# Rotary embedding on one core: tiles of 6, 5 and 5 positions without TensorE, and one 256 KB strip of a store split over partitions

## The chip, the cores and the metric

The kernel runs on one core of a Trainium2 chip. The metric is the device time of one execution in microseconds (us); lower is better. Five engines of the core appear in this text: TensorE (PE) multiplies matrices, VectorE (DVE) and GpSimd (POOL) work element by element, ScalarE (ACT) copies and scales, and SyncE (SP) issues the loads. The stores are issued from ScalarE's queue. All transfers between HBM and the on-chip memory (SBUF) run on the same 16 DMA engines. PSUM is a second on-chip memory, into which TensorE writes and which DVE and ScalarE can read and write.

## What is computed

`x` has 8 batches of 2048 positions, with 8 heads of 64 float32 values at each position; `cos` and `sin` have 32 values for each position.

```python
def reference(x, cos, sin):
    x1 = x[..., : x.shape[-1] // 2]
    x2 = x[..., x.shape[-1] // 2 :]
    cos = cos[None, :, None, :]
    sin = sin[None, :, None, :]
    out1 = x1 * cos - x2 * sin
    out2 = x1 * sin + x2 * cos
    return np.concatenate([out1, out2], axis=-1)
```

Both halves of a head are multiplied by the same cosines; to this is added the other half times the sine, with a minus sign for the first half. So an element costs two products and one addition. A batch of `x` is 4 MB; 33.6 MB are read and as many written.

## The kernel before

**Tiling.** A batch is laid over the 128 partitions: partition q holds 16 consecutive positions, 512 values each, so a row of 8192 values (32 KB). One SBUF tile `xt` (lines 64 to 71) holds a batch; there are five such buffers (`NBUF = 5`). The results are written over the input in `xt`, and the store reads it from there. The load of batch b+5 therefore has to wait until the store of batch b has landed and frees the buffer (lines 201 and 202).

**Loads and stores.** SyncE issues the loads in order: batch 0 in three parts (4, 4 and 8 positions), the two tables behind the first of them (lines 66 to 70), then one transfer of 4 MB for each batch. ScalarE's queue issues the stores (line 74): batch 0 in shares of 1, 7 and 8 positions, batch 7 in shares of 8, 4 and 4, every other batch in one of 16 (lines 186 to 191).

**Tables.** ScalarE builds `sgn` from the sines, once with a minus sign and once without (lines 89 to 91). The cosines are copied to PSUM as `cos_ps` (line 94) and the sines as `sin_ps` (line 92). `eye` and `neye` (lines 79 to 88 and 93) are an identity matrix and its negative.

**The work on a tile.** `rotate` (lines 115 to 177) works on a tile of 4 positions, of 2 at the beginning of batch 0 and at the end of batch 7 (lines 179 to 184). It comes in three kinds:

- "A", for all tiles but five: GpSimd multiplies the swapped halves by the signed sines into `t2` (line 134); DVE multiplies by the cosines into `t1`, which lies in PSUM and has one buffer (line 141); DVE adds the two into `xt` (line 148).
- "B", for the first tile of batches 2, 4 and 5: the products are the same, but `t1` lies in SBUF, TensorE adds the two by multiplying both with the identity into a PSUM tile `o` (lines 153 and 154), and ScalarE copies the sum to `xt` (line 155).
- "C", for the first tile of batches 1 and 3: DVE makes both products (lines 141 and 158), TensorE adds them with `eye` or `neye` (lines 169 and 170), ScalarE copies (line 174), and GpSimd has no part in it.

`t2` has three buffers, so GpSimd can be up to three tiles ahead of DVE's additions.

**Order.** `keep` holds the instructions of an engine in the order in which the program names them, so each queue is in program order. The loop in lines 193 to 202 goes over the batches and over the tiles of each; a share is stored as soon as the last tile in it is done.

Of the kernel before, what the change touches and what calls it, by code (L numbers as in the profile page):

```python
# [9 lines left out]
@with_exitstack  # L10
def kernel(
    ctx: ExitStack,
    tc: tile.TileContext,
    x: bass.AP,
    cos: bass.AP,
    sin: bass.AP,
    out: bass.AP,
):
    nc = tc.nc
    keep = tc.keep_in_program_order  # L20
    f32 = mybir.dt.float32
    PSUM = bass.MemoryType.PSUM

    B, S, H, D = x.shape
    Dh = D // 2
    P = 128
    HD = H * D
    R = S // P
    ROW = R * HD
    UNIT = 4 * HD  # L30
    NBUF = 5
    C = 512
    last = B - 1

    xv = x.rearrange("b (q r) h d -> b q (r h d)", q=P)
    ov = out.rearrange("b (q r) h d -> b q (r h d)", q=P)
    cos_src = cos.rearrange("(q r) d -> q r d", q=P)
    sin_src = sin.rearrange("(q r) d -> q r d", q=P)

    const_pool = ctx.enter_context(tc.tile_pool(name="const", bufs=1))  # L40
    tab_pool = ctx.enter_context(tc.tile_pool(name="tab", bufs=1, space=PSUM))
    t1_pool = ctx.enter_context(tc.tile_pool(name="t1p", bufs=1, space=PSUM))
    o_pool = ctx.enter_context(tc.tile_pool(name="op", bufs=2, space=PSUM))
    t1s_pool = ctx.enter_context(tc.tile_pool(name="t1s", bufs=2))
    xpool = ctx.enter_context(tc.tile_pool(name="xpool", bufs=NBUF))
    t2_pool = ctx.enter_context(tc.tile_pool(name="t2p", bufs=3))

    cos_sb = t1s_pool.tile([P, R, Dh], f32, tag="t1s", name="cos_sb")
    sin_sb = t1s_pool.tile([P, R, Dh], f32, tag="t1s", name="sin_sb")
    sgn = const_pool.tile([P, R, 2, Dh], f32, tag="sg")  # L50
    eye = const_pool.tile([P, P], f32, tag="eye")
    neye = const_pool.tile([P, P], f32, tag="neye")
    cos_ps = tab_pool.tile([P, R, Dh], f32, tag="cp")
    sin_ps = tab_pool.tile([P, R, Dh], f32, tag="sp")

    xts = {}

    def spans(sizes):
        lo = 0
        for n in sizes:  # L60
            yield lo, n
            lo += n

    def load(b):
        xt = xpool.tile([P, ROW], f32, tag="xt", name=f"xt{b}")
        for lo, n in spans([UNIT, UNIT, 2 * UNIT] if b == 0 else [ROW]):
            keep(nc.sync.dma_start(out=xt[:, lo : lo + n], in_=xv[b, :, lo : lo + n]))  # L67
            if b == 0 and lo == 0:
                keep(nc.sync.dma_start(out=cos_sb, in_=cos_src))  # L69
                keep(nc.sync.dma_start(out=sin_sb, in_=sin_src))  # L70
        xts[b] = xt

    def store(b, lo, n):
        keep(nc.scalar.dma_start(out=ov[b, :, lo : lo + n], in_=xts[b][:, lo : lo + n]))  # L74

    for b in range(NBUF):
        load(b)

    nc.gpsimd.memset(eye, 0.0)  # L79
    nc.gpsimd.affine_select(  # L80
        out=eye,
        in_=eye,
        compare_op=mybir.AluOpType.not_equal,
        fill=1.0,
        base=0,
        pattern=[[-1, P]],
        channel_multiplier=1,
    )
    for lo, hi in ((0, 4), (4, R)):
        keep(nc.scalar.mul(sgn[:, lo:hi, 0, :], sin_sb[:, lo:hi, :], -1.0))  # L90
        keep(nc.scalar.copy(sgn[:, lo:hi, 1, :], sin_sb[:, lo:hi, :]))  # L91
    keep(nc.scalar.copy(sin_ps, sin_sb))  # L92
    keep(nc.scalar.mul(neye, eye, -1.0))
    keep(nc.vector.tensor_copy(cos_ps, cos_sb))  # L94

    def rep(a, n):
        return dataclasses.replace(a, ap=[a.ap[0][:], a.ap[1][:], [0, n], a.ap[-1][:]])

    def swapped(a, nr):
        return dataclasses.replace(  # L100
            a,
            offset=a.offset + Dh,
            ap=[a.ap[0][:], [HD, nr], [D, H], [-Dh, 2], [1, Dh]],
        )

    def signed(a, nr):
        return dataclasses.replace(
            a, ap=[a.ap[0][:], [D, nr], [0, H], [Dh, 2], [1, Dh]]
        )

    kinds = {}
    for b, kind in ((1, "C"), (2, "B"), (3, "C"), (4, "B"), (5, "B")):
        kinds[(b, 0)] = kind

    def rotate(b, lo, n):
        kind = kinds.get((b, lo), "A")
        xt = xts[b][:, lo : lo + n]
        r0 = lo // HD
        nr = n // HD
        xk = xt.rearrange("p (r k d) -> p r k d", r=nr, d=Dh)  # L120
        xu = xt.rearrange("p (g u d) -> p g u d", u=2, d=Dh)
        if kind == "A":
            t1 = t1_pool.tile([P, n], f32, tag="t1")
        else:
            t1 = t1s_pool.tile([P, n], f32, tag="t1s")
        if kind == "C":
            t2 = t1s_pool.tile([P, n], f32, tag="t1s")
        else:
            t2 = t2_pool.tile([P, n], f32, tag="t2")
        t1u = t1.rearrange("p (g u d) -> p g u d", u=2, d=Dh)  # L130
        t2u = t2.rearrange("p (g u d) -> p g u d", u=2, d=Dh)
        if kind != "C":
            keep(
                nc.gpsimd.tensor_mul(  # L134
                    out=t2.rearrange("p (r h u d) -> p r h u d", r=nr, h=H, u=2),
                    in0=swapped(xt, nr),
                    in1=signed(sgn[:, r0 : r0 + nr, :, :], nr),
                )
            )
        keep(  # L140
            nc.vector.tensor_mul(  # L141
                out=t1.rearrange("p (r k d) -> p r k d", r=nr, d=Dh),
                in0=xk,
                in1=rep(cos_ps[:, r0 : r0 + nr, :], 2 * H),
            )
        )
        if kind == "A":
            keep(nc.vector.tensor_add(out=xt, in0=t1, in1=t2))  # L148
        elif kind == "B":
            for j in range(n // C):  # L150
                o = o_pool.tile([P, C], f32, tag="o")
                cs = slice(j * C, (j + 1) * C)
                nc.tensor.matmul(o, eye, t1[:, cs], start=True, stop=False)  # L153
                nc.tensor.matmul(o, eye, t2[:, cs], start=False, stop=True)  # L154
                keep(nc.scalar.copy(xt[:, cs], o))  # L155
        else:
            keep(
                nc.vector.tensor_mul(  # L158
                    out=t2.rearrange("p (r k d) -> p r k d", r=nr, d=Dh),
                    in0=xk,  # L160
                    in1=rep(sin_ps[:, r0 : r0 + nr, :], 2 * H),
                )
            )
            G = C // Dh
            for u in range(2):
                for j in range(n // 2 // C):
                    o = o_pool.tile([P, C], f32, tag="o")
                    gs = slice(j * G, (j + 1) * G)
                    nc.tensor.matmul(o, eye, t1u[:, gs, u, :], start=True, stop=False)  # L169
                    nc.tensor.matmul(  # L170
                        o, eye if u else neye, t2u[:, gs, 1 - u, :], start=False, stop=True
                    )
                    keep(
                        nc.scalar.copy(  # L174
                            xu[:, gs, u, :], o.rearrange("p (g d) -> p g d", d=Dh)
                        )
                    )

    def pieces(b):
        if b == 0:  # L180
            return [2 * HD, 2 * HD, UNIT, UNIT, UNIT]
        if b == last:
            return [UNIT, UNIT, UNIT, 2 * HD, 2 * HD]
        return [UNIT] * 4

    def shares(b):
        if b == 0:
            return [HD, 7 * HD, 2 * UNIT]
        if b == last:
            return [2 * UNIT, UNIT, UNIT]  # L190
        return [ROW]

    for b in range(B):
        done = 0
        outs = list(spans(shares(b)))
        for lo, n in spans(pieces(b)):
            rotate(b, lo, n)
            done = lo + n
            while outs and sum(outs[0]) <= done:
                store(b, *outs.pop(0))  # L200
        if b + NBUF <= last:
            load(b + NBUF)

# [29 lines left out]
```

## Time and profile before

| | |
|---|---|
| time, median of 9 runs | 163.92 us (163.42 to 168.92) |
| time of the profiled execution | 163.92 us, span 162.0 us |
| DVE busy | 140.1 us, 66 instructions |
| POOL busy | 135.8 us, 38 instructions |
| PE busy | 45.9 us, 80 instructions |
| ACT busy | 15.1 us, 27 instructions |
| bytes moved by DMA | 67.64 MB, mean 418 GB/s |
| load queue (q1), store queue (q10) | 49.6% and 48.2% of 16 engines' span |

The span goes from the first to the last instruction; the rest of the time lies around it. The shares of busy time are averages over the whole span: whether an engine sets the time is seen only from what it waits for, stage by stage. Times in the views are counted from the start of the span. In a group of instructions, the columns are line, engine, operation, output and inputs with their shapes and count, then busy time, the mean of one in ns, and the idle time just before them with what ended it. In the chain of waits, a line is start, length and what. In the table by windows, a line is the window, its length, the busy time of PE, PEld, DVE, ACT and POOL with their counts, the granted TensorE clock, the DMA share and the GB/s. In the timeline, a line is start, length, engine, line, operation and operands.

### The profile page before, as it was taken

How to read it: one execution, taken by the hardware profiler on the slowest of the kernel's cores; microseconds unless marked ns; L12 is line 12 of the kernel's file. 1: busy time of each engine (PE TensorE's matmuls, PEld its weight loads, DVE VectorE, ACT ScalarE, POOL GpSimd, SP SyncE). 2: the span in 40 equal slices, each digit the busy share in tenths (PEclk: the TensorE clock that was granted, in tenths of full speed). 3: DMA queues.
4: the chain of work that ended last, by engine and by line, in shares of the span. 5: the costliest groups of instructions: out<-in, count | busy, mean ns of one | idle time of the engine just before them, and what ended most of it. 6: DMA issues, size and time to landing. Idle time of an engine off the chain costs nothing.

```text
span 162.0 us, 440 instructions
## 1 busy us (share of the span) xinstructions
PE 45.9 (28%) x80; PEld 18.5 (11%) x80; DVE 140.1 (86%) x66; ACT 15.1 (9%) x27; POOL 135.8 (84%) x38
## 2 busy tenths in 40 slices
PE   0000000499008930894039802990000000000000
PEld 0000000143003400341024201430000000000000
DVE  0458999999999999999999899999899998999900
ACT  3310000012100310022001400121000000000000
POOL 1199999999999799979995999996999969999100
PEclk9999999999755997589857995699655555555555
DMA  5999998899999999998999999999999999989994
GB/s 194 413 433 505 437 405 380 372 429 510 388 401 441 494 413 388 502 405 388 502 405 396 486 407 405 477 413 421 469 405 453 453 388 461 445 388 433 413 415 172
DMA packets 3457, 67.64 MB, mean 418 GB/s; under 512 B 384, under 2 KB 384, under 8 KB 768
## 3 DMA queue, kind: packets, MB, share of 16 engines
q1 hardware_dynamic: 1728, 34.08, 49.6%
q10 hardware_dynamic: 1728, 33.56, 48.2%
q14 instruction: 1, 0.01, 0.0%
HBM read 34.08 MB, written 33.55 MB: 418 GB/s over the span
## 4 chain that ended last, share of the span: by engine, by line
DMA 46%; DVE 36%; POOL 8%; issue 4%; SPq 1%; ACT 0%; DVEq 0%; POOLq 0%; ACTq 0%
DMA xt<-in_x_dram 24%; DVE t L141 18%; DMA out_dram<-xt 18%; DVE xt L148 16%; POOL t L134 8%; DMA sin_sb<-in_sin_dram 3%; DVE t L158 1%; SPq L69 0%; SPq L67 0%; ACT sgn L91 0%; DVEq L148 0%; ACT sgn L90 0%; POOLq L134 0%; ACTq L74 0%
## 5 line engine op out<-in xcount | busy, mean ns | idle before, releaser
L134 POOL TENSOR_TENSOR t<-xt,sgn 128x2048 f32<-128x2048 f32 (+1 forms) x32 | 135.1, 4250 | 13.9 <-ACT sgn L91 6.0
L141 DVE TENSOR_TENSOR t<-xt,cos_ps 128x2048 f32<-128x2048 f32 (+1 forms) x34 | 73.4, 2166 | 0.8
L148 DVE TENSOR_TENSOR xt<-t,t 128x2048 f32<-128x2048 f32 (+1 forms) x29 | 62.2, 2145 | 6.8 <-POOL t L134 3.8
L153 PE MATMUL o<-t,eye 128*128 128x512 f32 x24 | 15.5, 734 | 25.4 <-DVE t L141 25.4
L169 PE MATMUL o<-t,eye 128*128 128x512 f32 x16 | 11.6, 828 | 37.8 <-DVE t L141 37.8
L154 PE MATMUL o<-t,eye 128*128 128x512 f32 x24 | 14.7, 702 | 0.0
L155 ACT COPY xt<-o 128x512 f32<-128x512 f32 x12 | 7.0, 586 | 45.0 <-PE o L154 45.0
L153 PEld LDWEIGHTS o<-t,eye 128*128 128x128 f32 x24 | 5.6, 247 | 33.7 <-issue 33.7
L174 ACT COPY xt<-o 128x512 f32<-128x512 f32 x8 | 4.7, 586 | 44.4 <-DVE t L141 26.0
L169 PEld LDWEIGHTS o<-t,eye 128*128 128x128 f32 x16 | 3.8, 256 | 42.7 <-POOL t L134 30.5
L154 PEld LDWEIGHTS o<-t,eye 128*128 128x128 f32 x24 | 5.4, 227 | 7.4 <-issue 7.4
L94 DVE COPY cos_ps<-cos_sb 128x512 f32<-128x512 f32 x1 | 0.7, 695 | 6.1 <-DMA cos_sb<-in_cos_dram 6.1
L170 PE MATMUL o<-t,neye 128*128 128x512 f32 x8 | 5.5, 800 | 0.1
L158 DVE TENSOR_TENSOR t<-xt,sin_ps 128x2048 f32<-128x2048 f32 x2 | 4.6, 2281 | 0.0
L170 PE MATMUL o<-t,eye 128*128 128x512 f32 x8 | 4.1, 592 | 0.0
L170 PEld LDWEIGHTS o<-t,neye 128*128 128x128 f32 x8 | 2.2, 290 | 4.2 <-issue 4.2
L170 PEld LDWEIGHTS o<-t,eye 128*128 128x128 f32 x8 | 1.5, 190 | 1.9 <-issue 1.9
L90 ACT ACT_TABLE_LOAD x1 | 1.3, 1283 | 0.7 <-PEq L217 0.7
L90 ACT ACTIVATE sgn<-sin_sb 128x128 f32<-128x128 f32 (+1 forms) x2 | 0.8, 414 | 4.7 <-DMA sin_sb<-in_sin_dram 4.7
L91 ACT COPY sgn<-sin_sb 128x128 f32<-128x128 f32 (+1 forms) x2 | 0.8, 388 | 0.0
L92 ACT COPY sin_ps<-sin_sb 128x512 f32<-128x512 f32 x1 | 0.6, 579 | 0.0
L79 POOL MEMSET eye<- 128x128 f32 x1 | 0.2, 204 | 0.3 <-POOLq L217 0.3
(6 smaller groups left out, 1.0 us busy)
## 6 DMA issues: line engine op xcount, KB each, us to landing
xt<-in_x_dram SPq DMA_DIRECT2D x7, 4096.0 KB, 39.5
out_dram<-xt ACTq DMA_DIRECT2D x6, 4096.0 KB, 28.5
out_dram<-xt ACTq DMA_DIRECT2D x2, 2048.0 KB, 18.9
xt<-in_x_dram SPq DMA_DIRECT2D x2, 1024.0 KB, 5.9
xt<-in_x_dram SPq DMA_DIRECT2D x1, 2048.0 KB, 11.4
out_dram<-xt ACTq DMA_DIRECT2D x2, 1024.0 KB, 8.8
out_dram<-xt ACTq DMA_DIRECT2D x1, 1792.0 KB, 20.3
cos_sb<-in_cos_dram SPq DMA_DIRECT2D x1, 256.0 KB, 4.9
```

What stands on the lines that cost most here:

```text
L90: keep(nc.scalar.mul(sgn[:, lo:hi, 0, :], sin_sb[:, lo:hi, :], -1.0))
L91: keep(nc.scalar.copy(sgn[:, lo:hi, 1, :], sin_sb[:, lo:hi, :]))
L134: nc.gpsimd.tensor_mul(out=t2.rearrange("p (r h u d) -> p r h u d", r=nr, h=H, u=2), in0=swapped(xt, nr), in1=signed(sgn[:, r0 : r0 + nr, ...
L141: nc.vector.tensor_mul(out=t1.rearrange("p (r k d) -> p r k d", r=nr, d=Dh), in0=xk, in1=rep(cos_ps[:, r0 : r0 + nr, :], 2 * H),)
L148: keep(nc.vector.tensor_add(out=xt, in0=t1, in1=t2))
L153: nc.tensor.matmul(o, eye, t1[:, cs], start=True, stop=False)
L154: nc.tensor.matmul(o, eye, t2[:, cs], start=False, stop=True)
L155: keep(nc.scalar.copy(xt[:, cs], o))
L158: nc.vector.tensor_mul(out=t2.rearrange("p (r k d) -> p r k d", r=nr, d=Dh), in0=xk, in1=rep(sin_ps[:, r0 : r0 + nr, :], 2 * H),)
L169: nc.tensor.matmul(o, eye, t1u[:, gs, u, :], start=True, stop=False)
L170: nc.tensor.matmul(o, eye if u else neye, t2u[:, gs, 1 - u, :], start=False, stop=True)
L174: nc.scalar.copy(xu[:, gs, u, :], o.rearrange("p (g d) -> p g d", d=Dh))
```

## The change

All tiles become kind "A": GpSimd makes the sine product, DVE the cosine product and the addition. TensorE, the tiles `o`, the SBUF `t1`, `sin_ps`, `eye` and `neye` are gone. The tables as loaded, `cos_sb` and `sin_sb`, move to the pool of constants. Batch 0 keeps its tiles of 2, 2, 4, 4 and 4 positions; all others are cut in tiles of 6, 5 and 5, so `t1` and `t2` grow to 6 positions. Batch 7 is stored in shares of 6, 5 and 5 positions. Batch 5 (the sixth) is stored in shares of 15 positions and 1, and the share of 1 position (256 KB) goes out in six transfers over 80, 14, 12, 10, 8 and 4 partitions. Loads are as before. No instruction of TensorE's is left but the branches around the kernel.

```diff
-    UNIT = 4 * HD
     NBUF = 5
-    C = 512
...
-    o_pool = ctx.enter_context(tc.tile_pool(name="op", bufs=2, space=PSUM))
-    t1s_pool = ctx.enter_context(tc.tile_pool(name="t1s", bufs=2))
...
-    cos_sb = t1s_pool.tile([P, R, Dh], f32, tag="t1s", name="cos_sb")
-    sin_sb = t1s_pool.tile([P, R, Dh], f32, tag="t1s", name="sin_sb")
+    cos_sb = const_pool.tile([P, R, Dh], f32, tag="cb")
+    sin_sb = const_pool.tile([P, R, Dh], f32, tag="sb")
...
-    eye = const_pool.tile([P, P], f32, tag="eye")
-    neye = const_pool.tile([P, P], f32, tag="neye")
...
-    sin_ps = tab_pool.tile([P, R, Dh], f32, tag="sp")
...
+    loads = {0: [4, 4, 8]}
+    pieces = {0: [2, 2, 4, 4, 4]}
+    stores = {0: [1, 7, 8], 5: [15, 1], last: [6, 5, 5]}
+    strips = {(5, 15): [80, 14, 12, 10, 8, 4]}
...
-    keep(nc.scalar.copy(sin_ps, sin_sb))
-    keep(nc.scalar.mul(neye, eye, -1.0))
...
-        kind = kinds.get((b, lo), "A")
...
+        keep(
+            nc.gpsimd.tensor_mul(
+                out=t2.rearrange("p (r h u d) -> p r h u d", r=n, h=H, u=2),
+                in0=swapped,
+                in1=signed,
             )
+        )
         keep(
             nc.vector.tensor_mul(
-                out=t1.rearrange("p (r k d) -> p r k d", r=nr, d=Dh),
-                in0=xk,
-                in1=rep(cos_ps[:, r0 : r0 + nr, :], 2 * H),
+                out=t1.rearrange("p (r k d) -> p r k d", r=n, d=Dh),
+                in0=xt.rearrange("p (r k d) -> p r k d", r=n, d=Dh),
+                in1=cosines,
             )
         )
-        if kind == "A":
-            keep(nc.vector.tensor_add(out=xt, in0=t1, in1=t2))
-        elif kind == "B":
...
+        keep(nc.vector.tensor_add(out=xt, in0=t1, in1=t2))
...
     for b in range(B):
-        done = 0
-        outs = list(spans(shares(b)))
-        for lo, n in spans(pieces(b)):
+        outs = list(spans(stores.get(b, [R])))
+        for lo, n in spans(pieces.get(b, [6, 5, 5])):
             rotate(b, lo, n)
-            done = lo + n
-            while outs and sum(outs[0]) <= done:
-                store(b, *outs.pop(0))
+            while outs and sum(outs[0]) <= lo + n:
+                so, sn = outs.pop(0)
+                cs = slice(so * HD, (so + sn) * HD)
+                for p0, p1 in spans_of(strips.get((b, so), [P])):
+                    keep(
+                        nc.scalar.dma_start(out=ov[b, p0:p1, cs], in_=xts[b][p0:p1, cs])
+                    )
```

More of the change, by code (lines that the diff above doesn't have):

```diff
@@ L42 @@
     t1_pool = ctx.enter_context(tc.tile_pool(name="t1p", bufs=1, space=PSUM))
-    o_pool = ctx.enter_context(tc.tile_pool(name="op", bufs=2, space=PSUM))
-    t1s_pool = ctx.enter_context(tc.tile_pool(name="t1s", bufs=2))
     xpool = ctx.enter_context(tc.tile_pool(name="xpool", bufs=NBUF))
     t2_pool = ctx.enter_context(tc.tile_pool(name="t2p", bufs=3))
-    cos_sb = t1s_pool.tile([P, R, Dh], f32, tag="t1s", name="cos_sb")
-    sin_sb = t1s_pool.tile([P, R, Dh], f32, tag="t1s", name="sin_sb")
+    cos_sb = const_pool.tile([P, R, Dh], f32, tag="cb")
+    sin_sb = const_pool.tile([P, R, Dh], f32, tag="sb")
     sgn = const_pool.tile([P, R, 2, Dh], f32, tag="sg")
-    eye = const_pool.tile([P, P], f32, tag="eye")
-    neye = const_pool.tile([P, P], f32, tag="neye")
     cos_ps = tab_pool.tile([P, R, Dh], f32, tag="cp")
-    sin_ps = tab_pool.tile([P, R, Dh], f32, tag="sp")
-    xts = {}
+    loads = {0: [4, 4, 8]}
+    pieces = {0: [2, 2, 4, 4, 4]}
+    stores = {0: [1, 7, 8], 5: [15, 1], last: [6, 5, 5]}
+    strips = {(5, 15): [80, 14, 12, 10, 8, 4]}
     def spans(sizes):
@@ L62, in spans, with spans_of @@
             lo += n
+    def spans_of(sizes):
+        for lo, n in spans(sizes):
+            yield lo, lo + n
+    xts = {}
     def load(b):
         xt = xpool.tile([P, ROW], f32, tag="xt", name=f"xt{b}")
-        for lo, n in spans([UNIT, UNIT, 2 * UNIT] if b == 0 else [ROW]):
-            keep(nc.sync.dma_start(out=xt[:, lo : lo + n], in_=xv[b, :, lo : lo + n]))
+        for lo, n in spans(loads.get(b, [R])):
+            cs = slice(lo * HD, (lo + n) * HD)
+            keep(nc.sync.dma_start(out=xt[:, cs], in_=xv[b, :, cs]))
             if b == 0 and lo == 0:
@@ L71, in load @@
         xts[b] = xt
-    def store(b, lo, n):
-        keep(nc.scalar.dma_start(out=ov[b, :, lo : lo + n], in_=xts[b][:, lo : lo + n]))
     for b in range(NBUF):
         load(b)
[L79 to L88, printed above, removed]
     for lo, hi in ((0, 4), (4, R)):
@@ L91 @@
         keep(nc.scalar.copy(sgn[:, lo:hi, 1, :], sin_sb[:, lo:hi, :]))
-    keep(nc.scalar.copy(sin_ps, sin_sb))
-    keep(nc.scalar.mul(neye, eye, -1.0))
     keep(nc.vector.tensor_copy(cos_ps, cos_sb))
[L96 to L103, printed above, removed]
-        )
@@ L106, in signed @@
-    def signed(a, nr):
-        return dataclasses.replace(
-            a, ap=[a.ap[0][:], [D, nr], [0, H], [Dh, 2], [1, Dh]]
-        )
[L111 to L115, printed above, removed]
-        kind = kinds.get((b, lo), "A")
[L117 to L121, printed above, removed]
-        if kind == "A":
[L123 to L138, printed above, removed]
@@ new lines, in rotate @@
+    def rotate(b, lo, n):
+        xt = xts[b][:, lo * HD : (lo + n) * HD]
+        t1 = t1_pool.tile([P, n * HD], f32, tag="t1")
+        t2 = t2_pool.tile([P, n * HD], f32, tag="t2")
+        part = xt.ap[0]
+        swapped = dataclasses.replace(
+            xt,
+            offset=xt.offset + Dh,
+            ap=[part[:], [HD, n], [D, H], [-Dh, 2], [1, Dh]],
+        )
+        s = sgn[:, lo : lo + n, :, :]
+        signed = dataclasses.replace(
+            s, ap=[s.ap[0][:], [D, n], [0, H], [Dh, 2], [1, Dh]]
+        )
+        c = cos_ps[:, lo : lo + n, :]
+        cosines = dataclasses.replace(
+            c, ap=[c.ap[0][:], c.ap[1][:], [0, 2 * H], c.ap[-1][:]]
+        )
[4 more added lines that the diff above has]
+                in1=signed,
@@ L139, in rotate @@
             )
+        )
         keep(
             nc.vector.tensor_mul(
-                out=t1.rearrange("p (r k d) -> p r k d", r=nr, d=Dh),
-                in0=xk,
-                in1=rep(cos_ps[:, r0 : r0 + nr, :], 2 * H),
-            )
-        )
-        if kind == "A":
-            keep(nc.vector.tensor_add(out=xt, in0=t1, in1=t2))
-        elif kind == "B":
[L150 to L171, printed above, removed]
-                    )
[L173 to L193, printed above, removed]
-        done = 0
-        outs = list(spans(shares(b)))
-        for lo, n in spans(pieces(b)):
-            rotate(b, lo, n)
-            done = lo + n
-            while outs and sum(outs[0]) <= done:
-                store(b, *outs.pop(0))
+                out=t1.rearrange("p (r k d) -> p r k d", r=n, d=Dh),
@@ new lines, in rotate @@
+                in0=xt.rearrange("p (r k d) -> p r k d", r=n, d=Dh),
+                in1=cosines,
+            )
+        )
+        keep(nc.vector.tensor_add(out=xt, in0=t1, in1=t2))
+    for b in range(B):
+        outs = list(spans(stores.get(b, [R])))
+        for lo, n in spans(pieces.get(b, [6, 5, 5])):
+            rotate(b, lo, n)
+            while outs and sum(outs[0]) <= lo + n:
[4 more added lines that the diff above has]
+                        nc.scalar.dma_start(out=ov[b, p0:p1, cs], in_=xts[b][p0:p1, cs])
+                    )
```

## The prediction, made before the changed kernel was run

> **What bounds the kernel now.** I read the totals first, then the chain of waits, then the end of the run in short windows, then the busy engines instruction by instruction.
>
> ```profile
> span 162.0 us, 440 instructions
> ...
> PE 45.9 (28%) x80; PEld 18.5 (11%) x80; DVE 140.1 (86%) x66; ACT 15.1 (9%) x27; POOL 135.8 (84%) x38
> ...
> DMA  5999998899999999998999999999999999989994
> ...
> q14 instruction: 1, 0.01, 0.0%
> ```
>
> The DMA row is at 9 or close to it from the second slice to the last but one: the transfers are the resource that is full. DVE and POOL are not far behind, at 86% and 84%.
>
> ```profile
> 62.99 29.58 DMA out_dram<-xt
> ...
> 92.65 39.49 DMA xt<-in_x_dram
> ...
> 132.28 4.52 POOL t L134
> ...
> 152.52 1.23 DVE xt L148
> ```
>
> This is the chain. Batch 2's store is issued at 62.99 and lands at 92.57; this frees a buffer, so batch 7's load is issued at 92.65 and lands at 132.14; only then do POOL and DVE turn to batch 7, and DVE is done at 153.75. So the DMA queues set the pace of the compute, and DVE waits for them.
>
> ```profile
> 158.00:159.00 1.00, 0.00 (x0) 0.00 (x0) 0.00 (x0) 0.00 (x0) 0.00 (x0) 0.50 1.08 459
> 159.00:159.50 0.50, 0.00 (x0) 0.00 (x0) 0.00 (x0) 0.00 (x0) 0.00 (x0) 0.50 0.66 279
> 159.50:160.00 0.50, 0.00 (x0) 0.00 (x0) 0.00 (x0) 0.00 (x0) 0.00 (x0) 0.50 0.28 115
> 160.00:160.50 0.50, 0.00 (x0) 0.00 (x0) 0.00 (x0) 0.00 (x0) 0.00 (x0) 0.50 0.08 33
> ```
>
> The last two numbers are the DMA share and GB/s. The queue is full until 159 although DVE stopped at 153.75: there was a backlog of stores. Then a share of 0.08, about one engine of sixteen, works on alone. The trace's landing marks say the same: of the last store's sixteen marks fifteen fall between 159.68 and 160.25 and one at 161.15. Batch 2's store and batch 5's load, landing near 92.5, have no such straggler (all marks within 0.55); batch 3's, landing near 113, have it. Between them lies the one instruction fetch of the run (q14), at 96.9. So that fetch put one DMA engine some 0.9 us behind, and a full engine never catches up.
>
> **The change, part by part.** The sum is made against the profiled execution: span 162.0, time 163.92, so 1.92 lies outside the span; its time equals the median of the nine runs. The last store lands at 161.15, leaving 0.85 to the span's end, which I keep.
>
> TensorE gone. Three "B" tiles had their addition on TensorE and ScalarE; it returns to DVE as 3 additions of 2.29. Two "C" tiles had sine products on DVE (L158, 2.28); these become additions of 2.29 there, and POOL gets 2 products of 4.52. The 20 ScalarE copies, sin_ps, neye and eye cost nothing now: ScalarE is 9% busy, and the last two constants are made while POOL waits for the sine table until 7.32. So DVE has 16 positions times two passes in every batch.
>
> Tiles of 6, 5 and 5.
>
> ```profile
> L141 DVE TENSOR_TENSOR t<-xt,cos_ps 128x2048 f32<-128x2048 f32 x30 | 68.5, 2292 | 0.7
> ...
> L141 DVE TENSOR_TENSOR t<-xt,cos_ps 128x1024 f32<-128x1024 f32 x4 | 4.9, 1228 | 0.1
> ...
> L134 POOL TENSOR_TENSOR t<-xt,sgn 128x2048 f32<-128x2048 f32 x28 | 125.9, 4522 | 7.9 <-DMA xt<-in_x_dram 5.0 <-DVE xt L148 2.9
> ...
> L134 POOL TENSOR_TENSOR t<-xt,sgn 128x1024 f32<-128x1024 f32 x4 | 9.3, 2346 | 6.0 <-ACT sgn L91 6.0
> ```
>
> ```profile
> 18.80 2.29 DVE L141 TENSOR_TENSOR t<-xt,cos_ps 128x2048 f32<-128x2048 f32 x1
> 21.20 2.29 DVE L148 TENSOR_TENSOR xt<-t,t 128x2048 f32<-128x2048 f32 x1
> 23.52 2.29 DVE L141 TENSOR_TENSOR t<-xt,cos_ps 128x2048 f32<-128x2048 f32 x1
> ...
> 148.59 1.23 DVE L141 TENSOR_TENSOR t<-xt,cos_ps 128x1024 f32<-128x1024 f32 x1
> 149.93 1.23 DVE L148 TENSOR_TENSOR xt<-t,t 128x1024 f32<-128x1024 f32 x1
> 151.19 1.23 DVE L141 TENSOR_TENSOR t<-xt,cos_ps 128x1024 f32<-128x1024 f32 x1
> ```
>
> A round of DVE (product, addition, gaps) takes 23.52 - 18.80 = 4.72 for 4 positions and 151.19 - 148.59 = 2.60 for 2, so 1.06 per position and 0.48 per round. No row shows a tile of 5 or 6 positions. Bounds for a batch: 4 x 4.72 = 18.88 if larger tiles save nothing, 16 x 1.06 = 16.96 if they cost no fixed part at all. I take the line through both rows: 6.84 + 5.78 + 5.78 = 18.40. POOL by its rows: 2.176 per 2 positions and 0.17 fixed, so 6.70 and 5.61; a batch 17.92, less than DVE.
>
> Then I walk the two engines through. Batch 0 keeps its pieces, so DVE ends it at 28.2 as before (the addition at 25.92 plus 2.29). POOL starts batch 1 at 25.6 and needs 6.70, so DVE's first addition waits to 32.3, 0.5 lost. Batch 1 ends at 47.2. From there DVE is never kept waiting: six batches of 18.40 give 65.6, 84.0, 102.4, 120.8, 139.2, 157.6. POOL starts batches 5, 6 and 7 near 97.4, 115.4 and 133.3, after the loads that landed at 92.4, 112.8 and 132.1 before. Before, DVE ended at 153.75; now 3.85 later.
>
> Do the later stores starve the queue? A full queue needed the stores of batches 1 to 6 by 53.6, 73.1, 92.6, 113.0, 132.3 and 141.8 (when its predecessor landed). They come at 47.2, 65.6, 84.0, 102.4, 120.8 and 139.2: all in time, the last by 2.6. So loads keep their times. After load 7 the fifteen punctual engines moved 48 positions in 160.25 - 131.12 = 29.13, which is 0.607 a position. The 43 positions ahead of the last store land by 131.12 + 43 x 0.607 = 157.2. The last store, 5 positions, is issued at 157.6 into an idle queue. That is the new wait: the backlog that hid DVE's end is used up.
>
> Its cost has no row of its own. The first load, on an idle queue, took 4.63 for 4 positions (0.74 to 5.37); one position more gives 5.24, an upper bound, since it also warmed up on reads. Lower bound: 1.0 to the first packet (as the first load), 5 x 0.607 of data, 0.35 from the last packet to landing (as the last store of before): 4.4. I take 4.8: landing at 162.4, so 1.25 later than 161.15.
>
> The instruction fetch. TensorE's stream was the long one; with it the fetch at 96.9 should go, and the straggler's 0.9 with it. This is a gain only for a kernel whose queue is full at the end. Here it shortens the idle stretch and is worth nothing; if the fetch stays, its engine is free near 158.1, still before the last store's data can start (158.6), so again nothing.
>
> The strip. Six transfers of 256 KB in all replace one share of a large store. ScalarE's queue issues at 0.34 each, with nothing behind them until batch 6's store at 139.2; they sit behind batch 5's large part, which lands near 140. All transfers take eight completion semaphores in turn, and each waits for the one eight before it: the sixth strip so waits for load 7 (131 to 132) and batch 6's store for batch 4's; behind them on ScalarE nothing is due before 139.2. Cost from below: nothing, as the gap before the last store hides over a microsecond. From above: five more transfers, each with the first load's whole start (4.63 - 4 x 0.607 = 2.2), 11 us. The nearest row is transfers queued behind each other: cosines, then sines, 256 KB each, landed at 6.03 and 6.71, 0.68 apart, where 0.607 is data. So 0.07 each, 0.35 for five, hidden: I take 0. The Trainium skill (DMA: Bandwidth & Descriptors, Anatomy of one DMA) speaks against the strip: it puts a fixed cost of about 2 us on every DMA, most of it the receipt of the write, and the same page's rules call transfers under 64 KB mostly overhead. Five more would then be an estimated 10 us; the 0.68 between cosines and sines shows no such cost for transfers queued together.
>
> Sum: 163.92 + 1.25 = 165.17, say 165.2.
>
> **The rivals.** Faster: DVE does the larger tiles cheaply, and the queue stays full. It decides if the last store is issued before about 155.7 (drained packets at 156.9, less 1.0 to the first, and 0.2 for the spread of the engines), 1.9 earlier than my 157.6, which asks for a batch in 18.13. Then the kernel ends as now without its straggler: 163.92 - 0.90 = 163.0. For it: DMA is the full resource today. Against it: two sizes of tile lie on a line, and the fixed part that could go is only 0.48 a round.
>
> No change: DVE ends 0.9 to 1.5 sooner than I say, so that the idle gap just eats what the lost straggler gives: 163.6 to 164.25.
>
> Larger tiles save nothing: 18.88 a batch puts DVE's end near 161.0, and the time at 168.6. For it: a scratch tile of 6 positions was never run. Against it: the linear rows.
>
> The strips stall: 11 us between batches 5 and 6 delay the drain to 168.2, and then 5 x 0.607 to a landing at 171.3: 174.0. It decides above about 1.5. Against it stands the 0.68.
>
> **How the numbers follow.** Forecast 0.80: 164.4 (DVE 0.4 sooner, last store 4.4) to 166.1 (DVE 0.5 later, 5.24). Faster rival 0.08, no change 0.06, larger tiles slower 0.04, strips 0.02. Differences under 0.2%, 0.33 us, can't be told from no change. So faster 0.08, same 0.06, slower 0.86. The range 163.9 to 166.3 leaves out the faster rival, half of the middle one and most of the two slow ones: 0.17.
>
> **What would show it.** DVE busy near 145.5 and POOL near 143.7 with DVE hardly idle from 32 on; rounds of 6.84 and 5.78; the last store's issue at 157.6 and its landing under 5.3 later; an idle DMA stretch of a microsecond or more before it; no q14 fetch, and landing marks within 0.6. I am wrong if the last store is issued by 156, or if DMA shares stay at 1 until the last store's data.

## The result, and the profile after

The changed kernel takes 165.03 us (median; the kernel before 163.75 in all its runs): the ratio to the kernel before is 1.0088, with a 95% interval of 1.0075 to 1.0102. It is slower by 0.9%. Some executions of most kernels are disturbed and some 2 to 9 us longer; the ratios here, and the medians of the experiments, leave them out.

The profiled execution took 165.10 us with a span of 163.3. Its totals, its DMA row and its groups of instructions by shape:

```profile
span 163.3 us, 224 instructions
DVE 145.5 (89%) x53; ACT 2.6 (2%) x5; POOL 142.5 (87%) x30
...
DMA  5999999999999999999999999999999999999975
...
q14 instruction: 1, 0.01, 0.0%
```

```profile
L103 POOL TENSOR_TENSOR t<-xt,sgn 128x2560 f32<-128x2560 f32 x14 | 78.1, 5604 | 0.0
L103 POOL TENSOR_TENSOR t<-xt,sgn 128x3072 f32<-128x3072 f32 x7 | 46.8, 6686 | 0.0
L110 DVE TENSOR_TENSOR t<-xt,cos_ps 128x2560 f32<-128x2560 f32 x14 | 39.6, 2828 | 0.5
...
L110 DVE TENSOR_TENSOR t<-xt,cos_ps 128x3072 f32<-128x3072 f32 x7 | 23.5, 3361 | 0.2
```

The new tile sizes lie on the line through the old ones: 6.69 and 5.60 on GpSimd, 3.36 and 2.83 on DVE. DVE went from 140.1 to 145.5 busy, and from 32.3 us on the chain of waits now belongs to it alone. Its sums by line, and its last pieces:

```profile
by line: DVE xt L116 38.8%; DVE t L110 36.7%; POOL t L103 13.2%; issue 3.3%; DMA sin_sb<-in_sin_dram 3.3%; DVEq L116 0.3%; SPq L72 0.3%; SPq L70 0.2%; ACT sgn L81 0.2%; ACT sgn L80 0.0%
...
32.30 3.37 DVE xt L116
35.69 2.84 DVE t L110
...
149.24 2.84 DVE xt L116
152.10 2.84 DVE t L110
...
155.03 2.83 DVE xt L116
```

No load and no store stands in the chain any more but the sine table at the start. From 32.3 to 157.9 it is one DVE instruction after another. The waits of the whole run say the same: GpSimd's waits for loads, 5.0 us in five places before, are gone, and what DVE still waits for GpSimd (total, times and longest, in us) is little:

```profile
DVE xt L116 <- POOL t L103: 2.8, 3, 1.7
```

What this does to the transfers is seen in the last microseconds. The columns are the window, its length, DVE, ACT and POOL busy, clock, DMA share and GB/s (TensorE has no columns, as it does nothing):

```profile
156.00:157.00 1.00, 1.00 (x1) 0.00 (x0) 0.00 (x0) 1.00 0.97 410
157.00:158.00 1.00, 0.86 (x1) 0.00 (x0) 0.00 (x0) 1.00 0.35 143
158.00:159.00 1.00, 0.00 (x0) 0.00 (x0) 0.00 (x0) 1.00 0.39 164
159.00:160.00 1.00, 0.00 (x0) 0.00 (x0) 0.00 (x0) 1.00 1.10 461
160.00:161.00 1.00, 0.00 (x0) 0.00 (x0) 0.00 (x0) 1.00 0.87 358
```

Between 157 and 159 the DMA engines are at 0.35 and 0.39: the stores have run out. The sixteen engines end their last packets one after the other between 157.0 and 158.0, and no packet moves again until 158.73. In the kernel before, the share from 158 to 159 was 1.08 (shown in the prediction), and from 157 to 158 it was 0.99 (here with the two columns of TensorE):

```profile
157.00:158.00 1.00, 0.00 (x0) 0.00 (x0) 0.00 (x0) 0.00 (x0) 0.00 (x0) 0.50 0.99 418
```

The last store is issued at 157.89, as soon as DVE is done (155.03 + 2.83), and lands at 162.37, 4.48 later. Before, the last store was issued 4.1 earlier and landed at 161.15.

### The profile page after: what moved, and what is told of

It reads as the page before. It is cut to its first block, busy times and chain, and to the rows that moved or that the text cites. A ratio compares the mean times of both kernels' runs of the same rounds, so it can differ in the third digit from the quotient of the medians.

```text
span 163.3 us, 224 instructions
## 1 busy us (share of the span) xinstructions
DVE 145.5 (89%) x53; ACT 2.6 (2%) x5; POOL 142.5 (87%) x30
## 4 chain that ended last, share of the span: by engine, by line
DVE 75%; POOL 13%; issue 3%; DMA 3%; SPq 0%; DVEq 0%; ACT 0%
DVE xt L116 39%; DVE t L110 37%; POOL t L103 13%; DMA sin_sb<-in_sin_dram 3%; DVEq L116 0%; SPq L72 0%; SPq L70 0%; ACT sgn L81 0%; ACT sgn L80 0%
## 5 line engine op out<-in xcount | busy, mean ns | idle before, releaser
L103 POOL TENSOR_TENSOR t<-xt,sgn 128x2560 f32<-128x2560 f32 (+3 forms) x26 | 142.3, 5520 | 7.1 <-ACT sgn L81 7.1
L116 DVE TENSOR_TENSOR xt<-t,t 128x2560 f32<-128x2560 f32 (+3 forms) x26 | 72.4, 2784 | 5.2 <-POOL t L103 2.8
L110 DVE TENSOR_TENSOR t<-xt,cos_ps 128x2560 f32<-128x2560 f32 (+3 forms) x26 | 72.5, 2787 | 0.9
```

The costliest lines, as they stand in the source:

```text
L103: nc.gpsimd.tensor_mul(out=t2.rearrange("p (r h u d) -> p r h u d", r=n, h=H, u=2), in0=swapped, in1=signed,)
L110: nc.vector.tensor_mul(out=t1.rearrange("p (r k d) -> p r k d", r=n, d=Dh), in0=xt.rearrange("p (r k d) -> p r k d", r=n, d=Dh), in1=cosines,)
```

## The experiments

Three explanations were to be told apart. Theory A: DVE's chain, and behind it a last store that meets an idle queue, set the end. Rival B: the transfers of the changed kernel, the strip above all, cost the time. Rival C: the larger tiles cost it. Medians are in us; a ratio is to the kernel before, run on the same chip beside the experiment.

### The parts of the change alone

The changed kernel with batch 5's store whole:

```diff
-    stores = {0: [1, 7, 8], 5: [15, 1], last: [6, 5, 5]}
-    strips = {(5, 15): [80, 14, 12, 10, 8, 4]}
+    stores = {0: [1, 7, 8], last: [6, 5, 5]}
+    strips = {}
```

> The changed kernel with batch 5's store whole again. Theory A (DVE's chain plus a last store that meets an idle queue set the end): DVE ends at 157.9 and the last store lands near 162.4 as with the strip; 165.0 us, within 0.3. Rival B (the strip and the way it loads the DMA engines cost the time): the 1.2 us come back, near 163.8.

Measured: 164.92, ratio 1.0081 (1.0057 to 1.0104). The strip is not what made the kernel slower; B falls for this kernel. In the profiled execution, of 166.38 us, DVE ends at 157.86, as with the strip.

The kernel before with no tile on TensorE:

```diff
-    for b, kind in ((1, "C"), (2, "B"), (3, "C"), (4, "B"), (5, "B")):
-        kinds[(b, 0)] = kind
```

> The kernel before with no tile on TensorE, still tiles of 4 and no strip. Theory A: DVE has 31 rounds of 4.72 or 2.60 behind batch 0, ends at 160.9, and the last store (4 positions, idle queue, 3.9 from issue to landing) lands at 164.8; 167.5 us. Rival B (the strip is the cost): at most 163.8. Rival C (tiles of 6 and 5 are the cost, not the additions moved to DVE): below 165.0.

Measured: 168.33, ratio 1.0290 (1.0268 to 1.0312). This is the largest part of the change: alone it costs 4.8 us, and the other parts give 3.3 of them back. DVE ends at 157.86 with the larger tiles and at 161.54 without. So they are a gain, and C falls. The time is 0.8 above the expectation, most of it on DVE's side: it ended at 161.54 instead of 160.9, for it began batch 1 0.2 later and stood still once for 0.5. The last store took 3.85 from issue to landing, as expected. The windows show the same picture as the changed kernel, more of it:

```profile
158.00:160.00 2.00, 1.97 (x2) 0.00 (x0) 0.00 (x0) 1.00 1.06 442
160.00:161.50 1.50, 1.40 (x2) 0.00 (x0) 0.00 (x0) 1.00 0.06 22
161.50:162.50 1.00, 0.04 (x1) 0.00 (x0) 0.00 (x0) 1.00 0.22 90
162.50:165.00 2.50, 0.00 (x0) 0.00 (x0) 0.00 (x0) 1.00 0.93 383
```

For one and a half microseconds the queue is all but idle (0.06) while DVE works on the last 2 of the 4 positions that the store carries.

### The last store and DVE's chain

The changed kernel with a smaller store at the end:

```diff
-    pieces = {0: [2, 2, 4, 4, 4]}
-    stores = {0: [1, 7, 8], 5: [15, 1], last: [6, 5, 5]}
+    pieces = {0: [2, 2, 4, 4, 4], last: [6, 5, 3, 2]}
+    stores = {0: [1, 7, 8], 5: [15, 1], last: [6, 5, 3, 2]}
```

> The changed kernel with batch 7 in tiles and stores of 6, 5, 3 and 2 positions. Theory A: DVE ends 0.5 later (158.35), but the store behind it has 2 positions instead of 5, which saves 1.8 of transfer; landing near 161.0, 163.7 us. Rival D (DVE's end is all that counts, the size of the last store doesn't): 165.5 us.

Measured: 163.93, ratio 1.0017 (1.0005 to 1.0029). DVE has more to do here, and the kernel is 1.1 us faster than the changed one. Rival D falls: what counts is DVE's end plus the transfer that has to follow it.

Two additions back on TensorE:

```diff
...
+    on_te = {(2, 6), (4, 6)}
...
-        t1 = t1_pool.tile([P, n * HD], f32, tag="t1")
+        te = (b, lo) in on_te
+        if te:
+            t1 = t2_pool.tile([P, n * HD], f32, tag="t2")
...
+        if te:
+            for j in range(n):
+                o = o_pool.tile([P, HD], f32, tag="o")
+                cs = slice(j * HD, (j + 1) * HD)
+                nc.tensor.matmul(o, eye, t1[:, cs], start=True, stop=False)
+                nc.tensor.matmul(o, eye, t2[:, cs], start=False, stop=True)
+                keep(nc.scalar.copy(xt[:, cs], o))
```

> The changed kernel with the second tile (5 positions) of batches 2 and 4 added on TensorE and copied by ScalarE, as kind B did. Theory A: DVE is freed of two additions, 5.8 us with their gaps; it then waits for batch 7's load, ends near 153.5, and the queue stays full to the end: 163.0 to 163.8 us. Rival B or C (strip or tile sizes cost the time): 165.0 us.

Measured: 174.63, ratio 1.0678 (1.0658 to 1.0698). A miss, and no test of the question: these tiles' `t1` takes one of the three buffers of `t2`, and TensorE and ScalarE work some 15 us on such a tile (56.9 to 71.9 for the first). Its waits (total, times and longest, in us):

```profile
DVE xt L141 <- POOL t L120: 19.4, 11, 3.4
...
POOL t L120 <- DVE xt L141: 12.8, 4, 3.5
```

GpSimd can no longer run as far ahead: it waits 12.8 us for DVE to free a buffer, and DVE then waits 19.4 for GpSimd. DVE does 6 us less work and ends 9.5 later, at 167.4. The lead that the third buffer gives is worth more here than the two additions.

The same relief without TensorE, by leaving the two additions out:

```diff
-        keep(nc.vector.tensor_add(out=xt, in0=t1, in1=t2))
+        if (b, lo) not in ((2, 6), (4, 6)):
+            keep(nc.vector.tensor_add(out=xt, in0=t1, in1=t2))
```

> The changed kernel without DVE's addition in the second tile (5 positions) of batches 2 and 4; these positions are stored as loaded. Theory A (DVE's chain and the last store behind an idle queue set the end): DVE has 5.8 us less, is then held by GpSimd and ends near 153, before the queue runs empty: 163.0 to 163.8 us. Rival B (the transfers of the changed kernel are the cost): 165.0 us.

Measured: 164.30, ratio 1.0027 (0.9990 to 1.0063). About half of the expected way back. The next kernel shows what kept the rest.

> The same with two additions left out, and batch 5's store whole. Here the queue is full to the end, so the strip alone is seen. Theory A (the strip's cost is a few tenths at most, either way): within 0.4 us of the kernel with the strip. Rival E (the strip's issue, 11 us in ScalarE's queue in the profile, or its uneven load holds the stores up): more than 0.4 us faster without it.

Measured: 163.40, ratio 0.9967 (0.9939 to 0.9994). With DVE relieved and the strip away the loss is gone; theory A holds. DVE ended at 155.24, 2.2 later than the 153 expected for the kernel just before, as it waited seven times for GpSimd (6.4 us in all); its last store was issued at 155.27, in time:

```profile
157.00:158.00 1.00, 0.00 (x0) 0.00 (x0) 0.00 (x0) 1.00 1.09 461
158.00:159.00 1.00, 0.00 (x0) 0.00 (x0) 0.00 (x0) 1.00 0.94 399
```

The dip of the changed kernel is filled. But between these two kernels lie 0.9 us, and they differ in the strip alone: on its cost in a kernel whose queue is full rival E's size was right, not A's. This doesn't show E's reason, the issue or the uneven load.

### The strip where the queue is full

The kernel before with the strip added:

```diff
+        cuts = [80, 14, 12, 10, 8, 4] if (b, lo) == (5, 15 * HD) else [P]
+        for p, m in spans(cuts):
...
+        if b == 5:
+            return [15 * HD, HD]
```

> The kernel before with batch 5's store in shares of 15 positions and 1, the 1 in six transfers over 80, 14, 12, 10, 8 and 4 partitions; nothing else changed. Theory A: 163.6 us, within 0.4, as the issues end before batch 6's store is due. Rival E: 164.2 us or more.

Measured: 164.63 beside 163.52, ratio 1.0038 (1.0005 to 1.0071). Rival E's size again: in a kernel that is bound by its transfers the strip costs time, 1.1 us by the medians and 0.1 to 1.2 by the ratio's interval.

A kernel meant to beat both, with GpSimd's idle end put to use:

```diff
-    pieces = {0: [2, 2, 4, 4, 4]}
+    pieces = {0: [2, 2, 4, 4, 4], 1: [4, 6, 6], last: [6, 5, 3, 2]}
...
+        on_pool = (b, lo) == (last, 14)
...
-        c = cos_ps[:, lo : lo + n, :]
+        c = (cos_sb if on_pool else cos_ps)[:, lo : lo + n, :]
...
-            nc.vector.tensor_mul(
+            (nc.gpsimd if on_pool else nc.vector).tensor_mul(
```

> The changed kernel with batch 7 in tiles and stores of 6, 5, 3 and 2, the cosine product of the last tile on GpSimd (done with its other work near 150), and batch 1 in tiles of 4, 6 and 6, so that DVE waits less for the first of them. Theory A: DVE ends near 156.6 and its last stores are issued before the queue is empty: 163.0 to 163.5 us, a little under the kernel before. Rival B: 164.5 us or more.

Measured: 164.04, ratio 1.0007 (0.9975 to 1.0040). DVE ends at 156.57 as expected, but the time is 0.5 to 1 above the expectation. Four more runs on one chip, this kernel itself and three variants of its strip, beside a kernel before of 163.66, ask why.

> The kernel with GpSimd's help and small last stores, but batch 5's store whole. If the strip costs 0.8 us wherever the queue is full (as the two pairs so far say), this takes 163.3 us, under the kernel before by 0.2%; if those pairs were chance, 164.1 as with the strip.

> As that with GpSimd's help, batch 5 stored in shares of 15 positions and 1, the 1 in one transfer of 128 partitions. Theory P (the small packets of 2 KB cost the time): 164.1 us as with the strip of six. Theories F (the number of transfers) and U (their uneven load on the DMA engines): 163.3 to 163.4 us, as without a strip.

> The same with the 1 position in six transfers over 48, 16, 16, 16, 16 and 16 partitions, so that each DMA engine can get 8 rows. Theory U (uneven load): 163.4 us. Theory F (number of transfers): 164.1 us.

> The kernel with GpSimd's help and the strip of 80, 14, 12, 10, 8 and 4 once more, on the same chip as its variants: 164.1 us, within 0.3.

| batch 5's share of 1 position | median | ratio |
|---|---|---|
| none, store whole | 163.55 | 1.0000 (0.9981 to 1.0019) |
| one transfer, 128 partitions | 163.58 | 1.0006 (0.9990 to 1.0022) |
| six transfers, 48 and five times 16 | 164.08 | 1.0020 (1.0000 to 1.0039) |
| six transfers, 80, 14, 12, 10, 8, 4 | 164.24 | 1.0032 (1.0014 to 1.0051) |

In one transfer the same small packets cost nothing (163.58), so theory P falls. Six transfers take 0.5 more even when their rows are spread evenly, which speaks for F; but the intervals of 164.08 and 163.58 overlap, so this is a hint and not shown. The 0.2 between the uneven and the even spread can't be told from nothing. The kernel without a strip came out 0.2 above its expectation. In the windows it is done a little sooner:

```profile
159.00:160.00 1.00, 0.00 (x0) 0.00 (x0) 0.00 (x0) 1.00 0.76 309
160.00:161.70 1.70, 0.00 (x0) 0.00 (x0) 0.00 (x0) 1.00 0.02 7
```

```profile
159.00:160.00 1.00, 0.00 (x0) 0.00 (x0) 0.00 (x0) 1.00 0.81 326
160.00:161.70 1.70, 0.00 (x0) 0.00 (x0) 0.00 (x0) 1.00 0.07 29
```

The first is without, the second with the six uneven transfers: the last landing marks (each DMA engine marks when its part of a transfer has landed) come at 160.85 and 161.23. These 0.4 are what those two executions differ by. The medians with this strip and without differ by 0.7 to 1.1 in the three pairs, and where the remainder comes from stays open.

The best version, GpSimd's help without a strip, is 1.5 us faster than the changed kernel and, by its interval, level with the kernel before, without TensorE.

## Why the prediction was right, point by point

The forecast was 165.2, the median is 165.03, and the mechanism is the one that was forecast.

**DVE's chain.** Right. Rounds of 6.85 and 5.79 against 6.84 and 5.78; end of DVE at 157.86 against 157.6. Nearly all of the difference is in the start: the sine table landed at 6.97 instead of 6.72, and everything after it is shifted by some 0.26. GpSimd's 142.5 stands against 143.7 (its overlapping instructions are counted once), DVE's 145.5 against 145.5.

**The new wait.** Right: the queue ran dry between 157.0 and 158.0, where 157.2 was forecast, and stood still until 158.73. The last store took 4.48, inside the bounds of 4.4 and 5.24; the 4.8 taken was 0.3 too long, which cancels the later start. It is therefore luck that the landing agrees so well, 162.37 against 162.4; the mechanism is not luck. The smaller last store and the two missing additions each confirm one half of it, the transfer behind DVE and DVE's chain. By the Trainium skill (DMA: Bandwidth & Descriptors, Anatomy of one DMA), whose fit is for transfers that GpSimd issues, the estimate for this store, which ScalarE issues, is 2.0 of fixed cost and 3.0 of data, 5.0 in all. The store measured 4.48, which leaves 1.45 beside 5 x 0.607 of data.

**The stores before it.** Right: the stores of batches 1 to 6 were issued at 47.3, 65.7, 84.2, 102.6, 121.0 and 139.5, within 0.3 of the list, and none left the queue empty. The loads kept ahead as forecast, but with less room: GpSimd came to batch 7 at 132.06 instead of 133.3, and its load had landed at 131.66.

**The instruction fetch.** Wrong in its cause, and without weight in the sum as foreseen. The step said that TensorE's stream was the long one and that the fetch would go with it. It is there in every profile of this study, at 104.8 in the new one, also where TensorE executes nothing. It comes when DVE has started 62 to 68 instructions (its semaphore waits counted), GpSimd 37 to 41 and SyncE 16 to 20, while ScalarE's count is 21 to 40 and TensorE's anything from 3 to 71. So it does not go with TensorE's stream; whose it is stays open. Hence the other half of that step also fell: no kernel lost the fetch, and a full queue without TensorE ends near 163.4 to 163.6 instead of 163.0. The marks of the stores before the last lie some 1 us and more apart in the new profile, where 0.6 was forecast; only the last store's, on idle engines, are within 0.2. The fetch does not explain this, for the marks lie 1.3 apart at 26 us already, long before it; what spreads them stays open.

**The strip.** The value, nothing, was right for this kernel (164.92 without it), but two numbers behind it were off. The issues do not take 0.34 each (least, median and longest of the stores' issues in ns):

```profile
L127 ACTq DMA_DIRECT2D out_dram<-xt x18: 338/350/2330, 11.2 to 157.9; - x18
```

The six took 1.74, 2.17, 1.24, 2.33, 2.15 and 0.64 by the trace, 10.3 of ScalarE's queue. The sixth (issued at 131.68) waited for load 7 (landed at 131.66), as the prediction said, and all were over at 132.3, before batch 6's store came at 139.5, so the cover named in the prediction held. And the price without cover, 0.07 a transfer, 0.35 for five, looks too small: the medians of the three pairs give 0.7 to 1.1. The rival of 11 us is refuted all the same, and so is the estimate of 10 us that the prediction made from the Trainium skill (DMA: Bandwidth & Descriptors, Anatomy of one DMA). What the section states is the time of one transfer that GpSimd issues, most of it the wait until the write is confirmed, and not a price to be added up for transfers that ScalarE queues behind each other. Here the last marks of the six parts all fall between 141.7 and 142.4.

## What to carry to other kernels

When the shared transfer queue bounds a kernel, ask how long each engine may run before the backlog of stores is used up: here DVE had some 2 us to spare by the prediction's sum, and the change moved its end by 4.1. Then the end is that engine's chain plus the last transfer, which nothing hides, so a smaller last piece can pay for more instructions (1.1 us here). A trick that costs nothing in one regime has to be tried again in the other: the strip is free where DVE sets the pace and costs 0.7 to 1.1 us, by the medians, where the queue does.

## What the runs showed that was not expected

Transfers issued right behind the store of 15 positions held ScalarE's queue for 1.2 to 2.3 us each instead of 0.34, the first five of the changed kernel, and for 0.45 to 2.3 over all profiles. The number of partitions does not decide it: 14 took 2.17, 8 took 2.15, 16 took 1.9 to 2.05 in the even spread, and the one transfer of 128 took 2.01, in a kernel that lost no time by it. Why they take so long stays open. By these times a compute instruction behind them would have waited some 10 us. When the parts land, between 140 and 142 us, the landing marks of the five small ones number 14, 12, 10, 8 and 4: as many DMA engines took part. This agrees with the Trainium skill (DMA: Bandwidth & Descriptors, Why a DMA increments its semaphore by 16 and not by 1), which takes the largest number up to 16 that divides the outer size on both sides. Each of the five has one more mark 9 to 15 us earlier, just behind the end of its issue.

After one fetch of 8 KB of instructions, 0.3 us long, one DMA engine stays some 1 us behind in the kernel before, 1.03 at 112.8 and still 0.91 at the end, as if a full queue left no gap in which to catch up. That the fetch is the cause is read from the timing alone. Two other profiles whose marks lie close together, those of the kernels with GpSimd's help without a strip and with it once more, show the same step: the marks of a transfer lie 0.54 and 0.36 apart before the fetch (at 103.9 and 103.8) and 1.1 apart behind it. In the other profiles they lie 1 us and more apart long before the fetch, so it can't be seen there.
